# The first input-projection tile by tiles of tokens, the norm's row copied by VectorE, the index keys rounded later

## The chip, the core and the metric

The kernel runs on one core of a Trainium2 chip. The metric is the device time of one execution in microseconds. The core has a matrix engine (TensorE, PE in the rows), a vector engine (VectorE, DVE), a scalar engine (ScalarE, ACT), a general engine (GpSimd, POOL) and a sync engine (SP), which issues most of the transfers. Each engine executes its own list of instructions in order and waits at semaphores for the others.

## What is computed

One inference step of a decoder layer for 528 prompt tokens (512 and 16 learned meta tokens) and 64 sample tokens, 592 in all, of width 1024. All tokens are normalised, and one wide input projection gives the parts of a state-space branch and of a sparse attention branch. What the change touches is the start of it: the norm, and the columns of the projection for the indexer (keys ki, queries qi, per-head weights wi) and for the step sizes dt:

```python
def rmsnorm(x, w):
    y = xf * lax.rsqrt(jnp.mean(xf * xf, axis=-1, keepdims=True) + NORM_EPS)
    return (y * w.astype(F32)).astype(x.dtype)

u = rmsnorm(h, norm1_w)
z, xbc, dt_raw, q, k, v, qi, ki, wi, g_ssm, g_attn = split_in(u @ w_in)

def indexer_scores(qi, wi, ki):
    s = jax.nn.relu(jnp.einsum('bqhd,bsd->bqhs', qi, ki) * IDX_DIM ** -0.5)
    return jnp.einsum('bqhs,bqh->bqs', s, wi * IDX_HEADS ** -0.5)
```

The scores choose 128 keys for each prompt token (256 for a sample token), and attention runs over these. The state-space scan, the gates, the output projection and a squared-ReLU MLP follow.

## The kernel before

The work is float32 split in two: every operand x is kept as a rounded part and the rest (xh and xl; `split`, L121 to L123), and a product is three products, hi by hi, hi by rest, rest by hi, accumulated in one PSUM bank (`mm3`, L140 to L145, eight blocks of 128 rows, so 24 products and 24 weight loads for a bank). `weights` (L125 to L133) loads 128 columns of a weight matrix (the raw tile `wr`, two buffers), rounds them on ScalarE (`wh`, L122) and forms the rest on VectorE (`wl`, L123); `wh` and `wl` have three buffers. `inproj` (L264) makes two banks "w" of 296 tokens (288 where the meta tokens aren't needed) with one weight tile.

The first stage, in the order of the text:

- L193 to L203: SP requests the norm's row `w1r`, five tiles of tokens `xt` (four of 128, one of 80) and the first weight tile `w0`, which has the indexer keys, the per-head weights and the dt columns.
- L205 to L208: TensorE spreads the row over 128 partitions (a product with ones), and a copy puts each half of it into `wrow` (`w1row` in the rows).
- L209 to L225, per tile of tokens: the square sum on ScalarE (L213), the reciprocal root on VectorE and GpSimd (L154, L155), the normalised tile `xn` on VectorE (L216), eight transposes on TensorE (L222) into banks "a" and "s", then `uh` on ScalarE (L224) and `ul` on VectorE (L225).
- L226 to L243: the query weights `wq0`, and small transposes of the convolution weights and state (cwr, nwr, scr).
- L316 to L334: the product of `w0` with all tokens, copied to `smT`; from it the index keys `kiT` (their second copy, on partitions 64 to 127, is a DMA, L320), and the token-major `sm_tok` by transposes (L326, L329). `dsm` (L488, text further down) needs the skip factors `dsr`, a small DMA of its own.
- L337 to L347: four query weight tiles, each with two banks of 288 tokens. A bank is read by four or five instructions: ScalarE's rounding (L344) and VectorE's rest (L345) for the upper and for the lower 64 rows in turn, and a copy of the sample tokens' queries (`qis`, L347). A bank is free for the next product when these are done.
- L348 to L350: `kS` and `kL`, the rounded part and the rest of the keys, and from L355 on the scores (L363, L364).

The text's order is not the engines' order. A scheduler takes the instructions that are ready by its own model of times, keeps the text's order as priority, and writes one list for each engine. So softplus steps of the dt columns (`X`, then L439 to L457) stand between the query tiles on ScalarE and VectorE. The block `issue_after` of the change keeps the instructions that it encloses behind a named instruction on the same engine.

Of the kernel before, what the change touches and what calls it, by code (L numbers as in the profile page):

```python
# [20 lines left out]
HT, HQ = 296, 288  # L21
C_Z, C_X, C_DT, C_Q, C_K, C_QI, C_KI, C_GS, C_GA = 0, 2048, 5120, 5152, 6176, 6688, 7200, 7272, 8296
# [48 lines left out]
def body(ctx, tc, a, o):  # L71
    nc = tc.nc
    SB, PS, DR = bass.MemoryType.SB, bass.MemoryType.PSUM, bass.MemoryType.DRAM
    act, dve, pool, pe, sy = nc.scalar, nc.vector, nc.gpsimd, nc.tensor, nc.sync
# [9 lines left out]
    def pst(tag):  # L84
        return psp.tile([128, 512], FT, tag=tag, name=tag, bufs=PSB[tag])
# [18 lines left out]
    def mis():  # L104
        alt[0] += 1
        return pst("as"[alt[0] % 2])

    def flat(t):
        return t.rearrange("p a b -> p (a b)")
# [11 lines left out]
    def split(raw, hi, lo, lo_eng=None):  # L121
        act.activation(hi, raw, AF.Copy)  # L122
        (lo_eng or dve).tensor_tensor(lo, raw, hi.bitcast(FT), op=OP.subtract)  # L123

    def weights(parts, at=None, lo_eng=None):  # L125
        raw = wp.tile([128, 8, 128], FT, tag="wr", name="wr", bufs=WB[0])
        lo, hi = [(at[0] if at else wp).tile([128, 8, 128], FR, tag=n, name=n, bufs=at[2] if at else WB[1])
                  for n in (at[1] if at else ("wl", "wh"))]
        for sel, src in parts:
            sy.dma_start(sel(raw), src)  # L130
        split(raw, hi, lo, lo_eng)
        return hi, lo

    def block(src, r0, c0, kt=8):
        return src[r0:r0 + 128 * kt, c0:c0 + 128].rearrange("(k p) c -> p k c", p=128)

    def whole(src, r0, c0):
        return weights([(lambda r: r, block(src, r0, c0))])

    def mm3(ps, w, xh, xl, c0, c1):  # L140
        hi, lo = w
        for k in range(8):
            for i, (p, q) in enumerate(((hi, xh), (hi, xl), (lo, xh))):
                x = q[k] if isinstance(q, list) else q[:, k, :]
                pe.matmul(ps[:, :c1 - c0], p[:, k, :], x[:, c0:c1], start=(k == 0 and i == 0), stop=(k == 7 and i == 2))  # L145
# [7 lines left out]
    def rstd_of(dst, ssq, n, cols, p=128):  # L153
        dve.tensor_scalar(dst, ssq, 1.0 / n, EPS, op0=OP.mult, op1=OP.add)  # L154
        pool.tensor_tensor(dst, dst, K("half")[:p, :cols], op=OP.pow)  # L155
# [10 lines left out]
    uh = up.tile([128, KD, NT], FR, name="uh")  # L166
    ul = up.tile([128, KD, NT], FR, name="ul")
# [12 lines left out]
    wrow = p0.tile([128, D], FT, name="w1row")  # L180
# [6 lines left out]
    def load_x(t, dst):  # L187
        if t < 4:
            sy.dma_start(dst, xp[128 * t:128 * t + 128])
        else:  # L190
# [8 lines left out]
    w0 = weights([(lambda r: r[:, :, 0:96], w_in[:, C_KI:C_KI + 96].rearrange("(k p) c -> p k c", p=128)),  # L199
                  (lambda r: r[:, :, 96:128], w_in[:, C_DT:C_DT + 32].rearrange("(k p) c -> p k c", p=128))], lo_eng=dve)  # L200
# [4 lines left out]
    for c in range(2):  # L205
        ps = mis()
        pe.matmul(ps, one, w1r[:, 512 * c:512 * c + 512], start=True, stop=True)
        act.copy(wrow[:, 512 * c:512 * c + 512], ps)  # L208
    for t in range(5):  # L209
        n = 128 if t < 4 else 80  # L210
        xt = xts[t]
        jk = p0.tile([128, D], FT, tag="jk", name="jk", bufs=1)
        act.activation(jk[:n], xt[:n], AF.Square, accum_out=ssq[:n, t:t + 1])  # L213
        rstd_of(rs[:n, t:t + 1], ssq[:n, t:t + 1], D, 1, n)
        xn = p0.tile([128, D], FT, tag="xn", name="xn", bufs=3)
        dve.scalar_tensor_tensor(xn[:n], xt[:n], rs[:n, t:t + 1], wrow[:n], op0=OP.mult, op1=OP.mult)  # L216
        for q in range(2):
            ps = mis()
            pv = ps.rearrange("p (k n) -> p k n", k=4)
            for i in range(4):  # L220
                k = 4 * q + i
                pe.transpose(pv[:, i, :n], xn[:n, 128 * k:128 * k + 128], idf[:n, :n])  # L222
            h_ = uh[:, 4 * q:4 * q + 4, 128 * t:128 * t + n]
            ch = act.activation(h_, pv[:, :, :n], AF.Copy)  # L224
            cl = dve.tensor_tensor(ul[:, 4 * q:4 * q + 4, 128 * t:128 * t + n], pv[:, :, :n], h_.bitcast(FT), op=OP.subtract)  # L225
    wq0 = weights([(lambda r: r, block(w_in, 0, C_QI))])  # L226
    sy.dma_start(cst[0][:, NF:], a["cst"][:, NF:KEPT])

# [2 lines left out]
    ps = mis()  # L231
# [3 lines left out]
    ps = mis()  # L235
# [3 lines left out]
    for q in range(2):  # L239
        ps = mis()  # L240
# [23 lines left out]
    def inproj(parts, n=HT, w=None):  # L264
        w = w or weights(parts)
        out = []
        for h in range(2):
            ps = pst("w")
            mm3(ps, w, uh, ul, h * n, h * n + n)
            out.append(ps)  # L270
        return out

    def in_cols(c0):
        return [(lambda r: r, block(w_in, 0, c0))]
# [7 lines left out]
    def plain(dst, ps, n=HT, func=AF.Copy, scale=1.0):  # L282
        for h in range(2):
            act.activation(dst[:, h * n:(h + 1) * n], ps[h][:, :n], func, scale=scale)
# [12 lines left out]
    with tc.tile_pool(name="p1", bufs=1, reuse_waits="tile") as p1:  # L297
# [15 lines left out]
            dve.tensor_scalar(idx2[:, :, h], ptx, 2.0, float(h), op0=OP.mult, op1=OP.add)  # L313
        sm_tok = p1.tile([128, 5, 128], FT, name="sm_tok")
        smT = p1.tile([128, NT], FT, name="smT")
        plain(smT, inproj(None, w=w0))  # L316
        kiT = p1.tile([128, NT], FT, name="kiT")
        dve.tensor_copy(kiT[0:64, 0:16], smT[0:64, 576:592])
        dve.tensor_copy(kiT[0:64, 16:592], smT[0:64, 0:576])
# [3 lines left out]
        ps = mis()  # L323
# [4 lines left out]
        ps = mis()  # L328
# [8 lines left out]
        qS = p1.tile([128, 8, NP], FR, name="qS")  # L337
        qis = p1.tile([128, 4, NS], FT, name="qis")
        for ct in range(4):
            ps = inproj(in_cols(C_QI + 128 * ct) if ct else None, n=HQ, w=None if ct else wq0)  # L340
            for h, (c0, c1) in enumerate(((0, HQ), (HQ, 512))):
                for e in range(2):
                    own, oth = slice(64 * e, 64 * e + 64), slice(64 - 64 * e, 128 - 64 * e)
                    act.copy(qS[own, 2 * ct + e, c0:c1], ps[h][own, 0:c1 - c0])  # L344
                    dve.tensor_tensor(qS[oth, 2 * ct + e, c0:c1], ps[h][own, 0:c1 - c0],  # L345
                                      qS[own, 2 * ct + e, c0:c1].bitcast(FT), op=OP.subtract)
            act.copy(qis[:, ct, :], ps[1][:, 512 - HQ:HQ])  # L347
        kS = p1.tile([128, 528], FR, name="kS")  # L348
        kL = p1.tile([128, 528], FR, name="kL")
        split(kiT[:, 0:528], kS, kL)  # L350


        wis = p1.tile([128, 4, 8], FT, name="wis")
# [1 line left out]
        for t in range(4):  # L355
            L = LT[t]
            sc = am[:, LO[t]:LO[t] + L]
            for h in range(8):
                lq = qS[:, h, 128 * t:128 * t + 128]
                r = p1.tile([128, 528], FT, tag="ri", name="ri", bufs=2)  # L360
                for c0, c1 in pieces(L):
                    ps = mis()
# [20 lines left out]
        ps = mis()  # L383
# [34 lines left out]
        for c0, c1 in pieces(1032):  # L418
            ps = pst("a")
# [38 lines left out]
        ps = mis()  # L458
# [10 lines left out]
        ps = mis()  # L469
# [3 lines left out]
        ps = mis()  # L473
# [6 lines left out]
        ps = mis()  # L480
# [8 lines left out]
        ps = mis()  # L489
# [5 lines left out]
        ps = mis()  # L495
# [13 lines left out]
        for kt in range(6):  # L509
            c0, n = ((128 * kt, 128) if kt < 4 else (512, 16) if kt == 4 else (528, 64))  # L510
            ps = pst("s")
# [10 lines left out]
        for kp in range(8):  # L522
# [6 lines left out]
            ps = inproj(parts, n=HQ)  # L529
# [495 lines left out]
    for q in range(4):  # L1025
# [7 lines left out]
        for m in range(8):  # L1033
            if m % 2 == 0:
                src = w_s[512 * q:512 * q + 512, 128 * m:128 * m + 256].rearrange("(k p) c -> p k c", p=128)
                w = [flat(x).rearrange("p (k c) -> p k c", k=4) for x in
                     weights([(lambda r: flat(r).rearrange("p (k c) -> p k c", k=4), src)])]
# [4 lines left out]
            for c0, c1 in HALVES:  # L1042
                ps = pst("w")
# [21 lines left out]
    for m in range(8):  # L1065
# [6 lines left out]
        w = weights(parts)  # L1072
        tg = p4a.tile([128, NQ], FT, tag="tga", name="tga", bufs=2)
        sy.dma_start(tg, d_g[1, m])
        for c0, c1 in HALVES:
            ps = pst("w")
# [108 lines left out]
    wrow = pn.tile([128, D], FT, name="wrow")  # L1185
# [180 lines left out]
    w = whole(w_up, 0, 384)  # L1366
# [59 lines left out]
```

## Time and profile before

| What | Value |
| --- | --- |
| three runs | 1466.32, 1468.53 (median), 1472.68 us |
| profiled execution | 1462.62 us |
| its span in the trace | 1460.8 us |
| TensorE products, weight loads | 1421.3, 1273.8 us busy |
| VectorE, ScalarE, GpSimd | 1100.5, 757.2, 328.8 us busy |
| mean granted TensorE clock | 0.989 |

Times in the rows are microseconds from the start of the span unless marked ns. A row of the timeline has the start, the duration, the engine, the line, the operation, the tiles (out<-in) with their shapes, the count, and in brackets the idle time ahead of it with what ended it. Rows of a product overlap: each has its pipeline's length, so the distance from start to start is the price of one in a dense run.

### The profile page before, as it was taken

The page shows a single profiled execution, that of the slowest core. Times are in us where ns is not written, and L with a number is a line of the kernel's source. Part 1 is how long each engine was busy: PE and PEld are TensorE (multiplying, and loading weights), DVE is VectorE, ACT ScalarE, POOL GpSimd, SP SyncE. Part 2 cuts the span into 40 slices and gives each one's busy share as a digit, 9 for nine tenths or more (in the row PEclk, how much of TensorE's full clock was granted, in tenths as well). Part 3 has the DMA queues.
Part 4 walks back from the last instruction along what each step waited for, and adds up shares of the span by engine and source line. Part 5 has one row for each costly group of instructions (what it writes and reads, how often), then busy time and mean ns, then how long its engine had stood idle before and what let it go on. Part 6 is the DMA issues. An engine that isn't in the chain of part 4 may idle for free.

```text
span 1460.8 us, 26653 instructions
## 1 busy us (share of the span) xinstructions
PE 1421.3 (97%) x9808; PEld 1273.8 (87%) x9808; DVE 1100.5 (75%) x2246; ACT 757.2 (52%) x1721; POOL 328.8 (23%) x479
## 2 busy tenths in 40 slices
PE   7999999999999999999999999999999999999997
PEld 6898999998887988889688988898798988888986
DVE  5799989999879676582645777765589887888774
ACT  5454265556666663542645777832364554445441
POOL 1100010437546334352422633100000000000001
PEclk9999999999999999999999999999999999999999
DMA  6424375778987877877974533235223223232312
GB/s 182 108 59 125 110 205 154 221 218 231 265 257 205 243 223 189 248 208 239 310 252 128 157 86 87 69 105 176 80 84 105 89 88 85 87 91 86 89 68 72
DMA packets 276380, 222.08 MB, mean 152 GB/s; under 512 B 39741, under 2 KB 239281, under 8 KB 276226
## 3 DMA queue, kind: packets, MB, share of 16 engines
q1 hardware_dynamic: 271002, 201.50, 48.4%
q0 software_dynamic: 5248, 18.88, 3.7%
q8 instruction: 77, 1.26, 0.4%
q14 instruction: 53, 0.43, 0.1%
HBM read 175.50 MB, written 44.07 MB: 150 GB/s over the span
## 4 chain that ended last, share of the span: by engine, by line
PE 81%; DVE 7%; DMA 6%; SPq 2%; ACT 2%; issue 2%; POOL 1%; DVEq 0%; POOLq 0%; ACTq 0%
PE w L145 27%; PE s L1181 15%; PE w L1046 7%; PE a L1306 6%; PE w L1306 4%; PE a L145 3%; PE s L1012 2%; PE s L878 2%; PE a L1181 1%; DMA wr<-in_w_ssm_proj_dram 1%; PE s L741 1%; PE a L1002 1%; PE a L901 1%; DMA bc<-d_ac 1%; PE s L753 1%
## 5 line engine op out<-in xcount | busy, mean ns | idle before, releaser
L145 PE MATMUL w<-uh,wh 128*128 128x288 f32 (+1 forms) x1168 | 358.7, 307 | 8.6 <-ACT qis L347 1.7
L145 PE MATMUL w<-uh,wl 128*128 128x288 f32 (+1 forms) x1168 | 355.1, 304 | 0.0
L145 PE MATMUL w<-ul,wh 128*128 128x288 f32 (+1 forms) x1168 | 352.6, 302 | 0.0
L145 PEld LDWEIGHTS w<-uh,wh 128*128 128x128 f32 x1168 | 223.2, 191 | 16.2 <-issue 4.1
L145 PEld LDWEIGHTS w<-ul,wh 128*128 128x128 f32 x1168 | 223.3, 191 | 2.9 <-issue 2.2
L145 PEld LDWEIGHTS w<-uh,wl 128*128 128x128 f32 x1168 | 222.3, 190 | 1.7 <-issue 1.0
L123 DVE TENSOR_TENSOR wl<-wr,wh 128x1024 fp32r<-128x1024 f32 x129 | 160.0, 1241 | 74.9 <-ACT wh L122 73.8
L122 ACT ACTIVATE wh<-wr 128x1024 fp32r<-128x1024 f32 x129 | 135.8, 1057 | 154.9 <-PE w L145 81.7
L1183 DVE TENSOR_TENSOR h<-h,s 128x512 f32<-128x512 f32 (+1 forms) x161 | 108.5, 680 | 58.5 <-PE s L1181 58.2
L1181 PE MATMUL s<-dh,hh 128*128 128x512 f32 (+1 forms) x302 | 119.1, 394 | 0.0
L1181 PE MATMUL s<-dl,hh 128*128 128x512 f32 (+1 forms) x302 | 118.8, 393 | 0.0
L155 POOL TENSOR_TENSOR rs<-rs,cst 128x1 f32<-128x1 f32 (+2 forms) x15 | 8.3, 551 | 418.7 <-DVE rs L154 418.6
L1181 PE MATMUL s<-dh,hl 128*128 128x512 f32 (+1 forms) x242 | 95.0, 393 | 0.0
L122 ACT ACTIVATE dh<-wr 128x1024 fp32r<-128x1024 f32 x38 | 39.9, 1059 | 75.6 <-PE s L1181 59.0
L1046 PE MATMUL w<-ysh,wh 128*128 128x288 f32 x256 | 78.5, 309 | 0.2 <-DVE ms L1051 0.2
L1046 PE MATMUL w<-ysh,wl 128*128 128x288 f32 x256 | 76.8, 300 | 0.0
L1046 PE MATMUL w<-ysl,wh 128*128 128x288 f32 x256 | 76.7, 300 | 0.0
L728 ACT ACTIVATE bc<-bc,acum 128x128 f32<-128x128 f32 (+1 forms) x160 | 48.5, 379 | 41.9 <-DMA bc<-d_ac 41.7
L590 DVE SCALAR_TENSOR_TENSOR ca<-rb,cwT,ca 128x616 f32<-128x616 f32 x72 | 68.8, 957 | 0.3
L1181 PEld LDWEIGHTS s<-dl,hh 128*128 128x128 f32 x302 | 56.7, 188 | 12.5
L1181 PEld LDWEIGHTS s<-dh,hh 128*128 128x128 f32 x302 | 56.7, 188 | 10.2 <-DVE h L1183 0.5
L740 DVE SCALAR_TENSOR_TENSOR bc<-bc,dts,cb 128x128 f32<-128x128 f32 (+1 forms) x160 | 56.9, 419 | 0.3
(492 smaller groups left out, 3707.9 us busy)
## 6 DMA issues: line engine op xcount, KB each, us to landing
wr<-in_w_in_dram SPq DMA_DIRECT2D x64, 512.0 KB
wr<-in_w_up_dram SPq DMA_DIRECT2D x32, 512.0 KB
wr<-in_w_down_dram SPq DMA_DIRECT2D x32, 512.0 KB
st<-in_state_ssm_dram SPq DMA_DIRECT2D x16, 512.0 KB
bc<-d_ac SPq DMA_DIRECT2D x32, 256.0 KB
out_dram<-st SPq DMA_DIRECT2D x16, 512.0 KB
wr<-in_w_ssm_proj_dram SPq DMA_DIRECT2D x16, 512.0 KB
EB<-d_ec SPq DMA_DIRECT2D x40, 128.0 KB
```

The source lines that it names most:

```text
L122: act.activation(hi, raw, AF.Copy)
L123: (lo_eng or dve).tensor_tensor(lo, raw, hi.bitcast(FT), op=OP.subtract)
L145: pe.matmul(ps[:, :c1 - c0], p[:, k, :], x[:, c0:c1], start=(k == 0 and i == 0), stop=(k == 7 and i == 2))
L590: dve.scalar_tensor_tensor(ca[:, 0:616], rb[:, k:k + 616], cwT[:, 24 * k + ct:24 * k + ct + 1], ca[:, 0:616], op0=OP.mult, op1=OP.add)
L728: act.activation(bc[:n, i, :n], bc[:n, i, :n], AF.Relu, scale=-1.0, bias=acum[:n, c, h0 + i:h0 + i + 1])
L740: dve.scalar_tensor_tensor(mt, mt, dts[:n, c, 8 * g + hh:8 * g + hh + 1], cb[:n, :n], op0=OP.mult, op1=OP.mult)
L878: pe.matmul(v[64 * hp:64 * hp + 64], QZ[:, hp, :], kk, start=True, stop=True)
L1012: pe.matmul(py[64 * e:64 * e + 64, 0:256], Vt[:, j, kv:kv + 64], PT[:, e, j], start=(j == 0), stop=False)
L1046: pe.matmul(ps[:, :HQ], p[:, k, mc], x[k][:, c0:c1], start=(k == 0 and i == 0), stop=(k == 3 and i == 2))
L1181: pe.matmul(ps, p, w[:, cc], start=(k == 0 and i == 0), stop=(k == len(ws) - 1 and i == len(terms) - 1))
L1183: dve.tensor_tensor(h2[:, t, cc], h2[:, t, cc], ps, op=OP.add)
L1306: pe.matmul(ps, p[:, k, :], q[:, k, :], start=(k == 0 and j == 0), stop=(k == 3 and j == 2))
```

## The change

```diff
@@ -205,7 +205,7 @@
     for c in range(2):
         ps = mis()
         pe.matmul(ps, one, w1r[:, 512 * c:512 * c + 512], start=True, stop=True)
-        act.copy(wrow[:, 512 * c:512 * c + 512], ps)
+        dve.tensor_copy(wrow[:, 512 * c:512 * c + 512], ps)
     for t in range(5):
@@ -223,6 +223,9 @@
             ch = act.activation(h_, pv[:, :, :n], AF.Copy)
             cl = dve.tensor_tensor(ul[:, 4 * q:4 * q + 4, 128 * t:128 * t + n], pv[:, :, :n], h_.bitcast(FT), op=OP.subtract)
+        if t == 0:
+            ps0 = [pst("w"), pst("w")]
+        mm3(ps0[t // 3][:, 128 * (t % 3):], w0, uh, ul, 128 * t, 128 * t + n)
     wq0 = weights([(lambda r: r, block(w_in, 0, C_QI))])
@@ -313,7 +316,8 @@
-        plain(smT, inproj(None, w=w0))
+        act.copy(smT[:, 0:384], ps0[0][:, 0:384])
+        act.copy(smT[:, 384:592], ps0[1][:, 0:208])
@@ -337,17 +341,22 @@
         for ct in range(4):
-            ps = inproj(in_cols(C_QI + 128 * ct) if ct else None, n=HQ, w=None if ct else wq0)
+            with tc.issue_after(ch.ins), tc.issue_after(cl.ins):
+                w = weights(in_cols(C_QI + 128 * ct)) if ct else wq0
+            ps = inproj(None, n=HQ, w=w)
...
-            act.copy(qis[:, ct, :], ps[1][:, 512 - HQ:HQ])
+            qc = act.copy(qis[:, ct, :], ps[1][:, 512 - HQ:HQ])
+            if ct == 1:
+                behind = qc
         kS = p1.tile([128, 528], FR, name="kS")
         kL = p1.tile([128, 528], FR, name="kL")
-        split(kiT[:, 0:528], kS, kL)
+        with tc.issue_after(behind.ins):
+            split(kiT[:, 0:528], kS, kL)
```

The norm's row is copied by VectorE. The product of `w0` is made in five pieces, one per tile of tokens, in the text right behind that tile's transposes; three pieces share one bank, two the other. The rounding of the later query weights stands behind the last tile's `uh` and `ul`, and the keys' rounding on ScalarE behind the second query tile's `qis` copy. The lists of the engines differ only up to the products with the K columns (128x296, the first at 65.50 us in the trace of before); behind that they hold the same instructions in the same order, and GpSimd's list is the same throughout. Lines of the changed kernel are three to nine higher than the same lines of before.

ScalarE, from the copy of the first product (smT) to the first query tile's rounding (qS). Before:

```order
L284 ACTIVATE smT<-w 128x296
L455 ACTIVATE an<-brow 128x32
L122 ACTIVATE wh<-wr 128x1024
L284 ACTIVATE smT<-w 128x296
L408 COPY kiP<-kiT 64x8
L344 CAST qS<-w 64x288 x2
L439 ACTIVATE e__1170<-X 128x160
L440 ACTIVATE e__1170<-e__1170 128x160
L122 ACTIVATE kS<-kiT 128x528
```

With the change:

```order
L122 ACTIVATE wh<-wr 128x1024
L319 COPY smT<-w 128x384
L320 COPY smT<-w 128x208
L417 COPY kiP<-kiT 64x8
L464 ACTIVATE an<-brow 128x32
L417 COPY kiP<-kiT 64x8
L448 ACTIVATE e__1242<-X 128x160
L350 CAST qS<-w 64x288
L449 ACTIVATE e__1242<-e__1242 128x160
L350 CAST qS<-w 64x288
```

The rounding of the third query tile's weights (wh), which needs the first tile's buffer, now stands ahead of both copies of smT; the second kiP copy, which reads the keys' DMA copy, and the exponential of X stand ahead of the first rounding of qS, and kS has left the place.

SP, its DMAs from the constants (cst) to the query weights. Before:

```order
L299 DMA cst_294<-in_cst_dram 128x585
L301 DMA pt<-in_page_table_dram 128x64
L303 DMA brow<-in_dt_bias_dram 128x32
L304 DMA brow<-in_a_log_dram 128x32
L486 DMA dsr<-in_d_skip_dram 32x1
L321 DMA d_wi<-smT 8x8x8
L130 DMA wr<-in_w_in_dram 128x8x128
L320 DMA kiT<-kiT 64x592
```

With the change:

```order
L302 DMA cst_416<-in_cst_dram 128x585
L304 DMA pt<-in_page_table_dram 128x64
L306 DMA brow<-in_dt_bias_dram 128x32
L307 DMA brow<-in_a_log_dram 128x32
L324 DMA kiT<-kiT 64x592
L325 DMA d_wi<-smT 8x8x8
L495 DMA dsr<-in_d_skip_dram 32x1
L130 DMA wr<-in_w_in_dram 128x8x128
```

The keys' copy has moved ahead of the weights (wr), and the skip factors (dsr) have moved behind the keys' copy and d_wi.

VectorE, from the skip factors' step (dsm) to the first rest parts of the queries (qS). Before:

```order
L488 TENSOR_SCALAR dsm<-cst_294,dsr 32x16
L311 CAST idx<-ptx 128x8
L313 TENSOR_SCALAR idx_283<-ptx 128x8 x2
L123 TENSOR_TENSOR wl<-wr,wh 128x1024
L318 COPY kiT<-smT 64x16
L319 COPY kiT<-smT 64x576
L327 COPY sm_tok<-s 128x512
L330 COPY sm_tok<-a 80x128
L345 TENSOR_TENSOR qS<-w,qS 64x288
L354 TENSOR_SCALAR wis<-sm_tok 128x32
L437 TENSOR_TENSOR X<-sm_tok,brow 128x160
L345 TENSOR_TENSOR qS<-w,qS 64x288
```

With the change:

```order
L497 TENSOR_SCALAR dsm<-cst_416,dsr 32x16
L331 COPY sm_tok<-s 128x512
L334 COPY sm_tok<-a 80x128
L363 TENSOR_SCALAR wis<-sm_tok 128x32
L446 TENSOR_TENSOR X<-sm_tok,brow 128x160
L461 TENSOR_SCALAR X<-X 128x160
L351 TENSOR_TENSOR qS<-w,qS 64x288
L453 TENSOR_SCALAR w__1246<-e__1242 128x160
L454 RECIPROCAL w__1246<-w__1246 128x160
L351 TENSOR_TENSOR qS<-w,qS 64x288
```

The copies of kiT have moved ahead of dsm, and the second rest part of the queries has moved behind the reciprocal of the softplus.

## Rows read from the trace of the kernel before

**Rows 1.** The page's first part: busy time of each engine, share of the span.

```profile
PE 1421.3 (97%) x9808; PEld 1273.8 (87%) x9808; DVE 1100.5 (75%) x2246; ACT 757.2 (52%) x1721; POOL 328.8 (23%) x479
```

**Rows 2.** View by windows, busy time of each engine; the second row names the columns.

```profile
core 0: us, PE busy (x) PEld busy (x) DVE busy (x) ACT busy (x) POOL busy (x), PEclk, DMA share, GB/s
...
40.00:44.00 4.00, 1.99 (x15) 1.69 (x13) 3.81 (x9) 2.70 (x8) 2.59 (x3) 1.00 0.36 87
44.00:48.00 4.00, 3.86 (x17) 3.86 (x18) 3.80 (x11) 0.38 (x2) 2.01 (x3) 0.57 0.57 181
...
66.00:1460.80 1394.80, 1368.41 (x9467) 1225.14 (x9465) 1059.80 (x2164) 726.29 (x1654) 315.39 (x459) 0.99 0.52 152
```

**Rows 3.** Timeline of the first 20 us: norm row, squares, xn, first weight tile's rest.

```profile
9.48 0.56 ACT L208 COPY w1row<-a 128x512 f32<-128x512 f32 x1
...
9.95 1.06 ACT L213 ACTIVATE jk<-xt 128x1024 f32<-128x1024 f32 x1
10.15 2.48 DVE L216 SCALAR_TENSOR_TENSOR xn<-xt,rs,w1row 128x1024 f32<-128x1024 f32 x2 [0.39 <-ACT w1row L208]
...
15.07 1.22 DVE L123 TENSOR_TENSOR wl<-wr,wh 128x1024 fp32r<-128x1024 f32 x1
```

**Rows 4.** Timeline of TensorE, 25 to 66 us: first rows of stages, and waits.

```profile
25.06 0.44 PE L222 MATMUL s<-cst,xn 80*128 80x80 f32 x4
...
27.46 0.40 PE L145 MATMUL w<-uh,wh 128*128 128x296 f32 x1
...
30.97 0.38 PE L145 MATMUL w<-uh,wh 128*128 128x288 f32 x1
...
37.78 0.30 PE L145 MATMUL w<-uh,wh 128*128 128x288 f32 x1
...
43.20 0.33 PE L363 MATMUL s<-kS,qS 128*128 128x144 f32 x1 [1.66 <-DVE qS L345]
...
44.14 0.58 PE L145 MATMUL w<-uh,wh 128*128 128x288 f32 x1 [0.49 <-ACT qis L347]
...
53.09 0.40 PE L145 MATMUL w<-uh,wh 128*128 128x288 f32 x1 [0.59 <-ACT qis L347]
...
65.50 0.30 PE L145 MATMUL w<-uh,wh 128*128 128x296 f32 x1
```

**Rows 5.** Timeline of TensorE near 813 us: narrow products in a dense run.

```profile
813.28 0.27 PE L981 MATMUL s<-KL,QS 128*128 128x144 f32 x1
813.39 0.27 PE L980 MATMUL s<-KS,QS 128*128 128x144 f32 x1
```

**Rows 6.** Timeline of ScalarE and VectorE, 30 to 39 us: durations of the steps.

```profile
30.89 1.06 ACT L122 ACTIVATE wh<-wr 128x1024 fp32r<-128x1024 f32 x1
...
34.67 0.69 DVE L327 COPY sm_tok<-s 128x512 f32<-128x512 f32 x1 [1.02 <-PE s L326]
...
35.59 0.45 DVE L345 TENSOR_TENSOR qS<-w,qS 64x288 fp32r<-64x288 f32 x1
...
36.16 0.32 DVE L437 TENSOR_TENSOR X<-sm_tok,brow 128x160 f32<-128x160 f32 x1
...
37.53 1.15 DVE L445 RECIPROCAL w__1174<-w__1174 128x160 f32<-128x160 f32 x1
```

**Rows 7.** Timeline of SP's DMA issues, and of the steps that waited for them.

```profile
0.73 0.34 SPq L193 DMA_DIRECT2D w1r<-in_norm_w_dram  x1
...
2.27 2.04 PE L207 MATMUL s<-w1r,one 1*128 1x512 f32 x2 [2.27 <-DMA w1r<-in_norm_w_dram]
...
26.62 0.38 SPq L486 DMA_DIRECT2D dsr<-in_d_skip_dram  x1
...
30.83 0.22 DVE L488 TENSOR_SCALAR dsm<-cst,dsr 32x16 f32<-32x16 f32 x1 [0.51 <-DMA dsr<-in_d_skip_dram]
...
33.74 0.53 SPq L320 DMA_DIRECT2D kiT<-kiT  x1
...
38.68 0.65 ACT L122 ACTIVATE kS<-kiT 128x528 fp32r<-128x528 f32 x1 [1.46 <-DMA kiT<-kiT]
```

## Prediction

> **What bounds the kernel now.** The page's first part comes first: TensorE is busy 97% of the span [rows 1]. The view by windows shows where the rest lies [rows 2]. After 66 us TensorE is busy 1368.4 of 1394.8 us at a granted clock of 0.99, so the work that follows the first stage is bound by TensorE; a first stage that ends earlier or later moves the end by about the same amount. The change only alters the order of instructions in this first stage: from the first product of the K columns on (128x296, at 65.50 us [rows 4]) TensorE's list is the same in both kernels. So I work out when that product starts, and compare it with 65.50.
>
> In the timeline of the first 20 us [rows 3] the reader is to see that the norm's row is complete only when ScalarE's second copy ends at 9.48 + 0.56, and xn follows at 10.15. The lower rounding part of the first weight tile (wl, 15.07 + 1.22 = 16.29) is the last thing that the first product needs. In TensorE's timeline [rows 4] the query weights' first product starts at 30.97, the second query tile's at 37.78; then TensorE sits 1.66 us for qS and 0.49 us for qis before 44.14. Behind these waits the granted clock falls: 0.57 in the stretch 44 to 48 with TensorE busy 1.99 of the 4 us before it, 1.00 before that [rows 2]. 1.2 and 2.4 GHz are the two levels, and half of the clock costs about 1.5 us there (some 14 products of 288 columns, at 1.2 GHz 0.24 us each in place of the 0.133 that 48 of them take in the 6.8 us from 30.97 to 37.78, less 0.45 for five transposes).
>
> **The change, step by step.**
>
> *Norm row on VectorE.* Two ScalarE copies of 0.56 us go [rows 3], two VectorE copies come; the nearest VectorE row is the 128x512 copy out of PSUM, 0.69 us [rows 6]. VectorE has no long work before 10.15, so they cost nothing. xn of the first token tile can start near 7 us in place of 10.15. But the second and third xn now stand behind the third tile's rstd, which needs the square at 9.95 (1.06 and its read-out); that square stood behind the copy that goes, so it may start 0.5 us sooner, if its tokens have landed. So xn number two starts between 10.7 and 11.2, two xn take 2.48 [rows 3], two rest parts of 0.6 to 0.69 each, then wl 1.22: wl ends at 15.6 to 16.2, against 16.29. The three microseconds gained at the front are lost again in VectorE's queue. I take **16.0**.
>
> *First tile's products by token tiles.* Before: 48 products of 296 columns. Now five times 24, of 128 columns (the last 80): 120 products and 120 weight loads. A product of 144 columns in a dense run starts 0.11 us after the one before [rows 5], while 288 columns take 0.133; a weight load goes with each, so narrower products hardly get cheaper. I take 0.11: 120 x 0.11 = 13.2 us, where 48 of 0.14 (24 of them from 27.46 to near 30.9 [rows 4]) made 6.7. The Trainium skill ("TensorE: Matmul & The Clock Gate", section "Back-to-back issue gap") gives about 81 ns for each 128-column pair of load and product in a sustained stream. By that figure the 120 products would take 9.7 us and the sum below would be 3.5 us smaller; the row is of this kernel's own operands, so it decides.
>
> TensorE's list from 16.0 on: three token tiles, the transposes of the fourth (8 x 0.11 = 0.9), then those of the fifth and the small ones, which took 27.46 - 25.06 = 2.4 before [rows 4] (0.8 of it, the last convolution-state transposes, now stands behind the product), then the last two token tiles. With 0.3 for the fourth tile's rest part and 0.5 for products at the lower clock at the beginning (bounds 0 and 2.6, none and all of one tile), the last product ends at 16.0 + 13.2 + 0.9 + 1.6 + 0.3 + 0.5 = **32.5**. It ended at about 30.9.
>
> *What stands behind it.* The first tile's buffer comes free only now, and ScalarE's rounding of the third query tile's weights waits for it: it stands ahead of both smT copies. 1.06 [rows 6] + 0.56 (the 128x512 copy of rows 3 for 384 columns) + three transposes 0.3: the query product starts at **34.45**, 3.5 later than 30.97. It runs 6.8 as before, to 41.25.
>
> *The chain to the first free query bank.* VectorE: wl of those weights 1.22 [rows 3], two short copies, then kiT near 35.9. The key copy's DMA leaves SP first, then d_wi, then dsr, which stood far ahead before (26.62) and was needed at 30.83. Now dsr leaves near 36.9, and VectorE's dsm waits for it, with sm_tok, wis, X and every qS part queued behind. Landing: bounds 1.5 us (w1r, 0.73 to 2.27, nothing else in flight) and 4.2 (dsr itself, behind big loads); the key copy took 4.9 [rows 7]. Only the 148 KB key copy is ahead of it now, so I stay nearer the short end: 2.2, landing at 39.1. From the start of sm_tok to the end of X passed 1.8 us, of which 0.45 was a subtraction that now stands later: 1.35, with dsm before it X is done at 40.7. The exponential, ScalarE's cast and the first subtraction follow in turn, 0.4 to 0.45 each by the subtraction's row; then a small step (0.25, an estimate from X's 0.32) and the reciprocal 1.15, and the second subtraction 0.45 [rows 6]: the bank is free at **43.8**. TensorE is ready at 41.25: **2.5 us idle**. ScalarE's key copies for the samples also wait for the key copy's DMA, which by the long end lands at 40.8, still with X.
>
> *The second query tile's other half.* Before it starts, VectorE does four softplus steps (0.3 each by X's row), a weights' rest part (1.22), three more such steps, and two subtractions with ScalarE's cast between (0.45 each); with the hand-overs and ScalarE's last short copy 4.4 us, so 48.2, against 47.0 when TensorE has done the first half: 1.2 us idle. From 37.78 to 44.14 was 6.36; now 41.25 to 48.2 is 6.95: **+0.6**.
>
> *Later rounding of the index keys.* ScalarE's 0.65 for kS and VectorE's part for kL, with the 1.46 us wait for the key copy [rows 7], leave this place; they come behind the second qis, where TensorE has 3.2 us of products. Cost and gain there: nothing beyond the waits already counted. Six score products (6 x 0.11) move behind 44.14, one of the two waits of 0.6 (the row at 53.09 is the first) falls away: **+0.1**. The clock: idle of 2.5 and 1.2 against 1.66 and 0.49, so I keep the 1.5 us of half clock as it was (bounds: none, or twice).
>
> *Query weights requested later* (and held behind the last token tile): the loads were landed long before use; VectorE's buffer release orders them anyway. Nothing. POOL's list is unchanged.
>
> **Sum:** 3.5 + 0.6 + 0.1 = +4.2 us, in round figures +4. The profiled execution took 1462.62 us (span 1460.8 plus 1.8 around it), so 1466.6 on its scale. The median of the three runs shown is 1468.53, 0.4% above that execution; on its scale I forecast **1472.5**. Differences of up to 0.5%, 7.3 us, can't be told from no change.
>
> **Rivals.**
>
> *Slower by more than 0.5%.* dsr lands as late as in the profile, 4.2 us after issue (41.1): 2.0 more idle. A TensorE that idles 4.5 us then runs through a second stretch at 1.2 GHz, another 1.6. 4.2 + 3.6 = +7.8, 1476. It decides when the landing passes about 40 us. For it: dsr's and kiT's own rows [rows 7]. Against: they had a 512 KB weight load just ahead.
>
> *No loss.* The landing takes 1.5 and the idle time is too short to lower the clock: 4.2 - 0.7 - 1.5 = +2; with wl at 15.6 and no lower clock at the beginning, +1: 1469.5 to 1470.5. If the casts also came in time, the 2.5 idle would go and the result would be 2 us faster. Against it stands the reciprocal between the two subtractions.
>
> *Narrow products are cheap.* At 0.081 us each (the figure cited above): 4.2 - 3.5 = +0.7, 1469. The row at 0.11 speaks against it.
>
> **How the numbers follow.** Forecast (+2.5 to +6.5) 0.55; slower rival 0.15, of which 0.13 past the 0.5% bound; no loss 0.22, of which 0.03 might go past the bound on the fast side; cheap narrow products 0.08. So faster 0.03, same 0.84, slower 0.13. The range takes in the case without loss and the slower one, plus the spread of the runs shown (1466.3 to 1472.7): 1464 to 1480. The forecast's own is 1470 to 1476.
>
> **What would show it.** Right: 128-column products 0.11 apart; xn at about 7; wl near 16; the last first-tile product near 32.5 and the first query product near 34.5; dsm waiting for dsr; a wait of more than 2 us on qS near 41 to 44, with a clock near 0.5 behind it; the K columns' first product at 69.5. Wrong: products at 0.08; a query product before 32; no wait on dsr; or a K product before 66, by which the prologue would have gained.

## The result, and the profile after

The changed kernel takes 1474.13 us (median of 22 runs, 1467.35 to 1489.05) against 1466.67 for the kernel before (22 runs, 1461.38 to 1476.83): a ratio of 1.0054, 95% interval 1.0036 to 1.0073. Two later sets of runs of it gave 1.0066 (1.0032 to 1.0099) and 1.0072 (1.0046 to 1.0097). So it is slower. The median's 0.54% is a little more than the 0.5% that I had set as the bound, and the interval reaches below it. The forecast was 1472.5 us and "no change that can be told".

The profiled execution took 1479.76 us, with a span of 1478.0. The first part of its page, which answers to [rows 1]:

```profile
PE 1436.7 (97%) x9880; PEld 1288.7 (87%) x9880; DVE 1096.0 (74%) x2248; ACT 754.6 (51%) x1719; POOL 329.0 (22%) x479
```

TensorE is busy for 15 us more, although the change adds no arithmetic. The windows of [rows 2], now:

```profile
40.00:44.00 4.00, 4.00 (x21) 4.00 (x20) 0.00 (x0) 0.00 (x0) 0.00 (x0) 1.00 0.22 63
44.00:48.00 4.00, 4.00 (x26) 3.87 (x26) 1.33 (x2) 1.66 (x3) 0.00 (x0) 1.00 0.00 0
...
66.00:1460.80 1394.80, 1368.89 (x9532) 1226.67 (x9531) 1055.68 (x2166) 729.41 (x1668) 311.84 (x455) 1.00 0.53 152
```

In the first of them only 19 products start in 4 us, 0.21 us each (the row's 21 takes in two that began before it), with VectorE and ScalarE idle. The column of the granted clock shows 1.00, and the products' own spacing contradicts it: this trace has no record of the level before its first change. The timeline of VectorE, which answers to [rows 3]:

```profile
7.08 1.28 DVE L216 SCALAR_TENSOR_TENSOR xn<-xt,rs,w1row 128x1024 f32<-128x1024 f32 x1
10.53 1.29 DVE L216 SCALAR_TENSOR_TENSOR xn<-xt,rs,w1row 128x1024 f32<-128x1024 f32 x1
...
14.66 1.22 DVE L123 TENSOR_TENSOR wl<-wr,wh 128x1024 fp32r<-128x1024 f32 x1
```

The timeline of TensorE, which answers to [rows 4]:

```profile
15.93 0.47 PE L145 MATMUL w<-uh,wl 128*128 128x128 f32 x1
16.20 0.41 PE L145 MATMUL w<-uh,wh 128*128 128x128 f32 x1
16.42 0.41 PE L145 MATMUL w<-ul,wh 128*128 128x128 f32 x1
...
45.59 0.41 PE L145 MATMUL w<-ul,wh 128*128 128x80 f32 x1
45.80 0.41 PE L145 MATMUL w<-uh,wl 128*128 128x80 f32 x1
48.20 0.59 PE L145 MATMUL w<-uh,wh 128*128 128x288 f32 x1
...
57.03 0.37 PE L145 MATMUL w<-uh,wh 128*128 128x288 f32 x1 [0.35 <-DVE qS L351]
61.90 0.40 PE L145 MATMUL w<-uh,wh 128*128 128x288 f32 x1 [1.43 <-ACT qis L353]
...
81.63 0.30 PE L145 MATMUL w<-uh,wh 128*128 128x296 f32 x1
```

The narrow products stand 0.21 us apart from 15.9 to 45.8, whether they have 128 or 80 columns. That is about twice the 0.11 of [rows 5], the lower of the two levels. The query product starts at 48.20 (30.97 in [rows 4]) and the first K product at 81.63 (65.50): 16.1 us later, of 17.2 in the span. The steps behind the narrow products, which answer to [rows 7]:

```profile
46.04 1.06 ACT L122 ACTIVATE wh<-wr 128x1024 fp32r<-128x1024 f32 x1 [10.48 <-PE w L145]
...
50.39 0.83 SPq L495 DMA_DIRECT2D dsr<-in_d_skip_dram  x1
...
52.42 0.22 DVE L497 TENSOR_SCALAR dsm<-cst,dsr 32x16 f32<-32x16 f32 x1 [1.94 <-DMA dsr<-in_d_skip_dram]
```

### The profile page after: what moved, and what is told of

The parts are those of the page before. It is cut to its first block, busy times and chain, and to the rows that moved or that the text cites. A ratio compares the mean times of both kernels' runs of the same rounds, so it can differ in the third digit from the quotient of the medians.

```text
span 1478.0 us, 26796 instructions
## 1 busy us (share of the span) xinstructions
PE 1436.7 (97%) x9880; PEld 1288.7 (87%) x9880; DVE 1096.0 (74%) x2248; ACT 754.6 (51%) x1719; POOL 329.0 (22%) x479
## 4 chain that ended last, share of the span: by engine, by line
PE 79%; DMA 9%; DVE 6%; ACT 2%; issue 1%; POOL 1%; SPq 1%; POOLq 0%; DVEq 0%; ACTq 0%
PE w L145 27%; PE s L1190 15%; PE w L1055 7%; PE a L1315 6%; PE w L1315 4%; PE a L145 3%; PE s L1021 2%; PE s L887 2%; DMA bc<-d_ac 2%; PE a L1190 1%; PE a L1011 1%; DMA st<-in_state_ssm_dram 1%; PE a L910 1%; PE s L750 1%; PE s L879 1%
## 5 line engine op out<-in xcount | busy, mean ns | idle before, releaser
L145 PE MATMUL w<-uh,wh 128*128 128x288 f32 (+3 forms) x1192 | 368.9, 309 | 6.5 <-ACT qis L353 2.0
L145 PE MATMUL w<-uh,wl 128*128 128x288 f32 (+3 forms) x1192 | 365.2, 306 | 0.0
L145 PE MATMUL w<-ul,wh 128*128 128x288 f32 (+3 forms) x1192 | 363.0, 305 | 0.0
L145 PEld LDWEIGHTS w<-uh,wh 128*128 128x128 f32 x1192 | 232.4, 195 | 13.6 <-issue 3.6
L145 PEld LDWEIGHTS w<-ul,wh 128*128 128x128 f32 x1192 | 232.3, 195 | 3.0 <-issue 2.2
L145 PEld LDWEIGHTS w<-uh,wl 128*128 128x128 f32 x1192 | 231.3, 194 | 1.7 <-issue 0.7
L1055 PEld LDWEIGHTS w<-ysh,wh 128*128 128x128 f32 x256 | 48.0, 188 | 5.5 <-DVE ms L1060 1.2
```

The source lines that it names most:

```text
L1055: pe.matmul(ps[:, :HQ], p[:, k, mc], x[k][:, c0:c1], start=(k == 0 and i == 0), stop=(k == 3 and i == 2))
```

## The experiments

Theory: the loss is the narrow products at the lower clock. Rival: it is the waits that the change moves (dsr, the keys' copy, the roundings). Where a single execution is looked at, I compare the start of the first K product, since the lists are the same behind it. From there to the end the profiles differ by up to 8.5 us (1394.4 to 1402.9 us; 1395.3 before); the section on the prediction says what is known of that. Times of the kernel before are 1467.0 us in the first set of four, 1466.93 in the second, 1466.81 in the third.

The edits do not separate the theory from the rival, because the orders that the rival is about move with the five pieces. In all five profiles with 120 narrow products (three of the change, the tiles alone, the wide products ahead) ScalarE rounds the third query tile's weights ahead of both smT copies, and dsr leaves behind the keys' copy. With the whole product, with two wide pieces and with three narrow and one wide piece the rounding stands between the two smT copies, and dsr leaves ahead of the keys' copy, as before. So the ratios show what the pieces cost together with these orders, and only the traces can divide it. From the first tile's last product to the query's first product pass 2.4 us in each of the five profiles, against 0.27 before: the moved orders cost 2.1 us there. From the query's first product to the K product pass 33.1 to 33.4 us, and 35.6 with the tiles alone, against 34.5 before, so behind it the moved waits add 1.0 us in one profile and nothing in the others. The rest of the lag stands ahead of the first tile's last product (30.70 before), among the narrow products and the transposes between them.

**The product whole again, the other parts kept.**

```diff
-        mm3(ps0[t // 3][:, 128 * (t % 3):], w0, uh, ul, 128 * t, 128 * t + n)
...
-        act.copy(smT[:, 0:384], ps0[0][:, 0:384])
-        act.copy(smT[:, 384:592], ps0[1][:, 0:208])
+        plain(smT, inproj(None, w=w0))
```

> The changed kernel with the first tile's product back in two halves of 296 columns; row copies, later rounding and held-back weights stay. Theory (width and clock): the 120 narrow products, 0.213 us each at 1.2 GHz in the changed kernel's trace, are the whole loss; so the K columns' first product comes near 65 us or before (81.6 in the changed kernel, 65.5 before) and the time is within 0.2% of the kernel before, or below it. Rival (the moved waits: the weights' rounding ahead of smT, dsr behind the key copy, the reciprocal between the query subtractions): the K columns stay at 70 us or later, ratio 1.003 or more.

Measured: 1463.32 us, ratio 0.9973 (0.9952 to 0.9995), K product at 63.50. TensorE's timeline:

```profile
42.26 0.40 PE L145 MATMUL w<-uh,wh 128*128 128x288 f32 x1 [1.95 <-ACT qis L349]
...
63.50 0.30 PE L145 MATMUL w<-uh,wh 128*128 128x296 f32 x1
```

SP's timeline:

```profile
27.88 0.52 SPq L491 DMA_DIRECT2D dsr<-in_d_skip_dram  x1
```

Without the tiles the rest of the change is no loss. But dsr leaves early again here, and the rounding is back between the smT copies, so the run does not clear the moved waits that its expectation names. Two waits between the query tiles are left, of 1.95 and 0.59 us; ScalarE's second copy of the keys (kiP), which waits for the keys' DMA, stands ahead of the roundings before the first of them.

**The tiles alone, in the kernel before.**

```diff
+        if t == 0:
+            ps0 = [pst("w"), pst("w")]
+        mm3(ps0[t // 3][:, 128 * (t % 3):], w0, uh, ul, 128 * t, 128 * t + n)
...
-        plain(smT, inproj(None, w=w0))
+        act.copy(smT[:, 0:384], ps0[0][:, 0:384])
+        act.copy(smT[:, 384:592], ps0[1][:, 0:208])
```

> The kernel before with the product by token tiles alone; row copies on ScalarE, keys rounded early, weights not held back. Theory (width and clock): nearly the whole loss is here, narrow products 0.21 us apart until wide ones follow, K columns near 80 us, ratio 1.004 or more. Rival (the moved waits): the loss needs the later rounding and the new order of transfers, so the ratio is 1.002 or less.

Measured: 1474.83 us, ratio 1.0059 (1.0036 to 1.0081), K product at 71.65. So the five pieces alone, with the orders that move with them, make the whole loss; the part of the rival that needs the later rounding of the keys falls. Of the 6.15 us at the K product the trace gives 3.0 to the stretch of the narrow products (the last starts at 33.68, 30.70 before), 2.1 to the orders behind it and 1.0 to the waits of the query tiles; dsr, issued at 38.27, is waited for here too (2.33 us on VectorE). And in this execution the narrow products were not slow from the start. TensorE's timeline, where the 80 columns begin:

```profile
28.72 0.29 PE L145 MATMUL w<-uh,wl 128*128 128x128 f32 x1
28.83 0.35 PE L145 MATMUL w<-uh,wh 128*128 128x80 f32 x1
28.98 0.42 PE L145 MATMUL w<-ul,wh 128*128 128x80 f32 x1
29.20 0.41 PE L145 MATMUL w<-uh,wl 128*128 128x80 f32 x1
```

and its windows:

```profile
24.00:28.00 4.00, 4.00 (x41) 3.71 (x40) 2.08 (x4) 1.88 (x6) 0.00 (x0) 1.00 0.76 218
28.00:32.00 4.00, 4.00 (x25) 4.00 (x24) 0.00 (x0) 0.00 (x0) 0.00 (x0) 0.61 0.02 2
32.00:36.00 4.00, 4.00 (x25) 3.87 (x26) 1.45 (x2) 1.66 (x3) 0.00 (x0) 0.50 0.00 0
```

The products are 0.112 us apart up to 28.7 and 0.211 from 28.98 on; the granted clock falls to 0.50 while TensorE is busy without a gap.

**Two wide pieces, 384 and 208 columns.**

```diff
-        mm3(ps0[t // 3][:, 128 * (t % 3):], w0, uh, ul, 128 * t, 128 * t + n)
+        if t == 2:
+            ps0 = [pst("w"), pst("w")]
+            mm3(ps0[0], w0, uh, ul, 0, 384)
+        if t == 4:
+            mm3(ps0[1], w0, uh, ul, 384, 592)
```

> The changed kernel with the first product in two pieces, 384 columns behind the third token tile and 208 behind the fifth: 48 products and weight loads in place of 120. Theory (width and clock): the clock rises within the first piece, products of 384 columns come at 0.16 to 0.18 us after at most some 12 at 0.32, the K columns come near 65 us, ratio 0.998 to 1.001. Rival (the moved waits): as these all stay, the K columns come at 70 us or later, ratio 1.003 or more.

Measured: 1468.97 us, ratio 1.0014 (0.9991 to 1.0038), K product at 64.23; the 208-column products stand 0.112 us apart, as the 128-column ones do at the upper level. Fewer, wider pieces take the loss away. The moved waits did not stay, as the expectation has it: dsr leaves at 28.61, ahead of the keys' copy, so the run does not decide between the two.

**Wide products ahead of the narrow ones.** This kernel adds 24 products of 512 columns whose result is overwritten.

```diff
+            pw = ps0[1].rearrange("p (k n) -> p k n", k=4)
+            for i in range(24):
+                pe.matmul(pw, w0[0][:, i % 8, :], uh[:, 4 * (i // 12):4 * (i // 12) + 4, 0:128], start=(i == 0), stop=(i == 23))
```

> The changed kernel with 24 products of 512 columns (their result is overwritten) ahead of the first narrow one; they add 5.2 us at 2.4 GHz, 10.2 at 1.2. It asks whether narrow products keep a clock that is up. If they do: wide ones 0.43 and then 0.22 us apart, narrow ones 0.11 apart behind them, K columns at 73 to 79 us (12.4 less for narrow ones, 5 to 10 more for wide ones). If they don't: narrow ones 0.11 for a few us and then 0.21 again, with a fall of the granted clock in the record, K columns at 84 us or later.

Measured: 1478.32 us (three runs), ratio 1.0090 (1.0055 to 1.0125), with 7 us of added products in it; K product at 77.08. TensorE's timeline:

```profile
35.35 0.31 PE L145 MATMUL w<-uh,wl 128*128 128x128 f32 x1
35.46 0.41 PE L145 MATMUL w<-uh,wh 128*128 128x128 f32 x1
35.67 0.41 PE L145 MATMUL w<-ul,wh 128*128 128x128 f32 x1
```

The clock was up when the narrow products began (0.111 apart from 22.6 on) and fell at 35.46, among products of 128 columns. So the fall does not need 80 columns. Each of the two cases expected came in half: the narrow products kept the clock for 12.9 us, with the K product where the first case has it, and then lost it.

**The row copies alone; the later rounding alone; the held weights alone** (three kernels, each the kernel before with one part of the change).

```diff
-        act.copy(wrow[:, 512 * c:512 * c + 512], ps)
+        dve.tensor_copy(wrow[:, 512 * c:512 * c + 512], ps)
```

> The kernel before with one edit: VectorE copies the two halves of the norm's row. Theory (the copies cost nothing, and what the front gains is lost again behind the third tile's reciprocal root in VectorE's queue): first K product at 65 to 65.5 us against 65.50, ratio 0.999 to 1.001. Rival (the gain of the variant with the whole product, K at 63.50, comes from the earlier norm row): K near 63.5, ratio near 0.9975.

```diff
+            if ct == 1:
+                behind = qc
...
+        with tc.issue_after(behind.ins):
+            split(kiT[:, 0:528], kS, kL)
```

> The kernel before with one edit: the keys' rounding (kS, kL) stands behind the second query tile's sample copy. Theory: the first wait on qS (1.66 us) shortens since neither kS nor kL stands ahead of it, one of the waits of 0.6 goes; K product at 63.5 to 64.5, ratio 0.997 to 0.999. If the gain of the variant with the whole product is from this part, it is its whole 2 us here; rival (the gain is from the row copies): K at 65.5 or later, ratio 1.0.

```diff
+            with tc.issue_after(ch.ins), tc.issue_after(cl.ins):
+                w = weights(in_cols(C_QI + 128 * ct)) if ct else wq0
+            ps = inproj(None, n=HQ, w=w)
```

> The kernel before with one edit: the later query weights are held behind the last tile's uh and ul. Theory (the buffers order them anyway): K product at 63 to 66, ratio 0.998 to 1.001. Rival (the 0.3% that the variant with the whole product gained came from here): K near 63, ratio 0.9975.

Measured, in this order: ratio 1.0012 (0.9988 to 1.0037), 1.0003 (0.9976 to 1.0029) and 1.0001 (0.9976 to 1.0026), K product at 63.34, 64.37 and 67.19. None can be told from no change. For the second I had expected a gain (0.997 to 0.999), with the K product where it came. The K product of the first was 2 us earlier than I expected, as its rival had it, while its time shows no gain; that of the third, 1.2 us behind its expected range, came after a wait of 3.06 us on qS that I had not expected. Which part the 0.3% of the variant with the whole product comes from stays open; intervals of 0.25% to either side are too wide for that.

**The whole product, and the second copies of the keys behind too** (twice).

```diff
+                with tc.issue_after(behind.ins):
+                    act.copy(kiP[64 * b2:64 * b2 + 64, 1024:1032], kiT[64 * b2:64 * b2 + 64, 528 + 8 * b:536 + 8 * b])
```

> The changed kernel with the first tile's product whole again, in two halves of 296 tokens, and with one more edit: ScalarE's second copies of the keys for the samples (kiP) stand behind the second query tile's sample copy as well, so that no instruction ahead of the qS roundings waits for the keys' DMA. Theory (the 1.95 us of idle near 42 us and the stretch at half clock behind it come from that wait): idle falls to 0.6 or less, the clock stays up or falls for less than 2 us, K product at 60 to 62, against 63.50 with the copies ahead; ratio to before 0.995 to 0.997. Rival (the next wait, on the reciprocal or the rest parts of VectorE, takes its place): idle of 1 to 2 stays, K at 63 to 63.5, ratio 0.997 to 0.998.

> The variant with the whole product and the keys' copies behind too, a second time, to see whether it beats the kernel before by more than its interval (0.9978, 0.9954 to 1.0002, the first time). If its first K product near 62 is what sets the difference, ratio 0.996 to 0.999 again; if the first result was chance, 0.999 to 1.001.

Measured: 1462.46 us, ratio 0.9978 (0.9954 to 1.0002), K product at 61.74; then 1461.81 us, 0.9972 (0.9953 to 0.9991), K product at 61.01. TensorE's timeline of the second:

```profile
41.04 0.40 PE L145 MATMUL w<-uh,wh 128*128 128x288 f32 x1 [0.85 <-ACT qis L349]
41.28 0.29 PE L145 MATMUL w<-ul,wh 128*128 128x288 f32 x1
...
61.01 0.30 PE L145 MATMUL w<-uh,wh 128*128 128x296 f32 x1
```

The wait is 0.85 in place of 1.95 (expected: 0.6 or less; the remaining chain goes through VectorE's rest parts), and the products behind it stand 0.13 us apart at once. This version beats both kernels, by 0.3% against the one before. That the copies add to it is not shown in the time, since the whole product without them has 0.9973; in the profiles they bring the K product 1.8 and 2.5 us forward. In the first of the two executions (wait 1.10) the clock fell all the same, among products of 296 columns and without idle time right ahead, 1.0 us behind the small transposes (scr). TensorE's timeline of it:

```profile
24.96 0.92 PE L242 MATMUL a<-cst,scr 24*128 24x24 f32 x12
...
26.74 0.30 PE L145 MATMUL w<-ul,wh 128*128 128x296 f32 x1
26.87 0.37 PE L145 MATMUL w<-uh,wl 128*128 128x296 f32 x1
27.04 0.45 PE L145 MATMUL w<-uh,wh 128*128 128x296 f32 x1
```

The products go from 0.14 to 0.25 us apart at 26.87, for 3.7 us.

**The change itself, a second and a third execution** (no edit).

> The changed kernel itself, to see a second execution of it. Theory (128-column products, each with its own weight load, do not raise the clock, whatever the execution): 0.21 us apart from 15 to 46 us again, K product near 81, time near 1474, ratio 1.005. Rival (it depends on the execution, as the spread of its times from 1467 to 1489 would allow): 0.11 us apart for a part of them, as with the tiles alone, K product near 70, and a profiled execution near 1470.

Measured: 1473.96 us. The theory as written fell. TensorE's timeline of that execution:

```profile
16.24 0.41 PE L145 MATMUL w<-uh,wh 128*128 128x128 f32 x1
16.45 0.41 PE L145 MATMUL w<-ul,wh 128*128 128x128 f32 x1
16.66 0.37 PE L145 MATMUL w<-uh,wl 128*128 128x128 f32 x1
16.87 0.28 PE L145 MATMUL w<-uh,wh 128*128 128x128 f32 x1
...
30.36 0.30 PE L145 MATMUL w<-uh,wl 128*128 128x80 f32 x1
30.47 0.41 PE L145 MATMUL w<-uh,wh 128*128 128x80 f32 x1
...
49.96 0.40 PE L145 MATMUL w<-uh,wh 128*128 128x288 f32 x1 [1.13 <-ACT qis L353]
...
69.70 0.30 PE L145 MATMUL w<-uh,wh 128*128 128x296 f32 x1
```

Up to 16.87 it runs like the first one (16.84 there), within 0.05 us. Then the products go from 0.21 to 0.11 apart, which they never did in the first, and fall back at 30.47. The K product is at 69.70.

> The changed kernel a third time. In two executions TensorE's list ran alike up to 16.84 us; there the clock rose in one of them (products 0.11 us apart) and stayed low in the other (0.21). Theory (which of the two happens is decided anew in each execution, so the times spread): either kind in the profile, 0.21 apart up to about 46 us and a K product near 80, or 0.11 apart and one near 70; its times between 1467 and 1489 with some above 1480. Rival (the first execution was a single outlier): 0.11 apart, K product near 70, all times below 1479.

Measured: 1479.39 us (1467.69 to 1484.58, 10 runs, 4 of them above 1480). TensorE's timeline:

```profile
16.27 0.41 PE L145 MATMUL w<-ul,wh 128*128 128x128 f32 x1
16.48 0.41 PE L145 MATMUL w<-uh,wl 128*128 128x128 f32 x1
...
34.23 0.28 PE L145 MATMUL w<-ul,wh 128*128 128x128 f32 x1
...
37.17 0.30 PE L145 MATMUL w<-ul,wh 128*128 128x128 f32 x1
37.28 0.41 PE L145 MATMUL w<-uh,wl 128*128 128x128 f32 x1
...
78.59 0.30 PE L145 MATMUL w<-uh,wh 128*128 128x296 f32 x1
```

A third course: slow for the first 72 products, fast from 34.23, slow again from 37.28, K product at 78.59. Of the 38 times of the changed kernel in its three sets 12 lie above 1479 us; of 118 times of the kernel before 1 does.

**The last two tiles as one piece of 208 columns**, the first three at 128.

```diff
-        mm3(ps0[t // 3][:, 128 * (t % 3):], w0, uh, ul, 128 * t, 128 * t + n)
+        if t < 3:
+            mm3(ps0[0][:, 128 * t:], w0, uh, ul, 128 * t, 128 * t + 128)
+        if t == 4:
+            mm3(ps0[1], w0, uh, ul, 384, 592)
```

> The changed kernel with the last two tiles of tokens as one product of 208 columns; the first three stay at 128 columns: 96 products in place of 120. Theory (the 80-column products lose the clock, the 128-column ones only keep it): where the clock rises at the start, no half clock from 29 us on, the query product about 1.8 + 2 us earlier, K product at 64 to 67; where it doesn't rise, 0.21 apart for the 72 narrow ones and a rise in the 208-column ones, K product at 73 to 76. Time 1468 to 1472, ratio 1.001 to 1.004. Rival (any such narrow stretch loses the clock later): half clock again behind the first 72 products, K product near 70.

Measured: 1467.49 us, ratio 1.0006 (0.9979 to 1.0033), K product at 73.70. TensorE's timeline:

```profile
41.09 0.41 PE L145 MATMUL w<-uh,wl 128*128 128x208 f32 x1
41.30 0.37 PE L145 MATMUL w<-uh,wh 128*128 128x208 f32 x1
41.51 0.28 PE L145 MATMUL w<-ul,wh 128*128 128x208 f32 x1
```

Here the clock stayed low for all 72 narrow products (0.218 apart) and rose at 41.51, among those of 208 columns; it did not fall again before the K product. This profiled execution was the slowest of its ten (1458.03 to 1474.05); the median is that of the kernel before, so most of the others probably had a faster first stage, which no profile shows. The rival can't be told from it, since the clock had not been up among the narrow ones. That it is the 80 columns that lose the clock is not borne out: two executions (with the wide products ahead, and the third of the change) lost it at 128. Nor is it shown that the width does it. In all four profiles that lost the clock among narrow products, the fall came 0.5 to 1.8 us behind the transposes that stand between the pieces. In the three of them where the clock was up early, it held through the first three tiles, 7 to 8 us of narrow products with at most three such transposes among them. The whole product lost it behind the same kind of transposes once (26.87 above). A run that moves the transposes away is missing.

## Why the prediction was right and wrong

The time was 0.11% above the forecast and inside its range. That it came so near is partly luck. The forecast stands on a base of 1468.53 us, 1.9 above the median of 22 runs, and the change itself was forecast at +4 and measured at +7.5 us. I gave 0.13 to a loss above 0.5%, and by the median that is what it was, by a way that no rival had.

- **Right: the front.** xn at 7.08, its second at 10.53, the rest of the first weights done at 14.66 + 1.22 = 15.9 (forecast 16.0): the microseconds gained by the row copies are lost again in VectorE's queue.
- **Right: the price of a narrow product at the upper clock.** 0.112 us, and 0.112 for 208 columns too; the six of 80 columns that ran at this level took 0.106. So from 80 to 208 columns the width hardly matters. The Trainium skill ("TensorE: Matmul & The Clock Gate", section "Back-to-back issue gap") has 81 ns for 128 columns; no run here shows it, and the rival that took it falls.
- **Right: what stands behind the first tile's products.** The rounding ahead of the smT copies and the transposes took 2.2 us from the last product's end to the query product (forecast 1.95). The second half of the second query tile waited 1.43 and 1.13 us in the first two executions (forecast 1.2).
- **Right: dsr.** It landed some 2.0 us after its issue (50.39 to 52.4; 38.68 to 40.6 in the second execution; forecast 2.2). The slower rival, by which a late dsr was to make the loss, falls, although its sign came out.
- **Wrong: "0.5 for products at the lower clock at the beginning (bounds 0 and 2.6, none and all of one tile)".** I took it for granted that a dense run of narrow products is at the lower level for a moment and at the upper level from then on. In the first execution all 120 stayed low: 120 x (0.213 - 0.11) = 12.4 us. K came 12.1 us later than forecast; that the two are so near hides more terms, since transposes and first query products at the lower clock cost some 3.5 us more, and the waits and the half clock of the next point some 3.5 less. In the third it was most of them. In the second, the mildest, the lower clock cost 0.8 at the start (7 products), 1.9 among the 80 columns (18 x 0.104) and 1.7 in the first query products (15 x 0.116, 36.50 to 40.25): 4.4 in place of 0.5. The upper bound should have been the whole run at twice its price.
- **Wrong, and hidden by that: the waits.** Of the 2.5 us of idle time ahead of the second query tile 0.35 was left in the first execution and none in the second. The chain through dsr took 8.8 us from the query product on in the first and at most 8.9 in the second (forecast 9.35), but TensorE's own 48 products took 8.3 and 8.6 in place of 6.8, the first 17 and 15 of them at the lower clock; and the stretch at half clock behind it (1.5 us kept) is missing: products 0.13 apart right after 49.96. So the second execution hits the forecast (69.70 against 69.5 for the K product) by luck, with two errors that cancel.
- **"A first stage that ends earlier or later moves the end by about the same amount"** held for the first execution (16.1 of 17.2). In the second, 4.2 at the K product became 11.4 in the span. One place is seen in the waits of TensorE, the state tile's load (st), up to 3.3 us at once near 310 us. In these profiles it goes with the pieces. Some 240 us behind the K product all five profiles with 120 narrow products have a wait on st of 2.4 to 3.3 us, where the nine others have none or up to 1.6. In four of the five (and in one of the nine, three narrow and one wide) the granted clock falls there too, to 0.5 for 3.4 to 6.8 us. In these four the stretch behind the K product takes 1402.0 to 1402.9 us, in the first execution of the change 1396.3, in the nine others 1394.4 to 1399.2. So the sum lacks a term behind the first stage; why the load is waited for longer stays open. The kernel before, with us in total, times and the longest:

```profile
PE a L684 <- DMA st<-in_state_ssm_dram: 0.7, 1, 0.7
```

The second execution of the change:

```profile
PE a L693 <- DMA st<-in_state_ssm_dram: 5.8, 4, 3.3
```

The twelve other profiles have 2.2 to 6.5 us in all, those with the whole product among them; the profile of before is the odd one, and its time lies 4 us below the median of its kernel. How much of the 7.5 us between the medians is the first stage and how much this stays open, as does what decides in each execution whether the clock rises.

## What to carry to other kernels

Splitting a product into narrow pieces to start it earlier can cost the clock for the whole run of pieces, not only their extra count. Keep the pieces few, since from 80 to 208 columns each costs the same (two pieces of 384 and 208 columns lost nothing that could be told here), and bound the lower-clock term by the whole run. An edit that splits a product also moves the engines' lists; compare them before a run is taken to leave the other parts as they were. Look at several executions before a single profile explains a difference, at a point behind which the instruction lists agree. An instruction that waits for a DMA, ahead of roundings that free a bank, can be moved behind them: the wait shrank from 1.95 to 1.10 and 0.85 us here, though the time did not show it.

## What was not expected of the hardware

- A dense run of TensorE products, each with its weight load, and the transposes among them ran at the lower of the two levels for 30 us (15.9 to 45.8), and mostly at the upper level in another execution of the same program that had been alike until 16.87.
- The level also fell during such a run, without idle time ahead of it: at 28.9, 30.5, 35.5 and 37.3 us in four executions, each time 0.5 to 1.8 us behind a block of transposes, and once at 26.9 among products of 296 columns.
- The granted-clock column reads 1.00 until the first recorded change. The profiled execution has a mean of 0.997 (0.989 before) and is the slower one; the spacing of the products shows the level.
